# Far-attention stores moved from SyncE's queue to GpSimd's, and larger yields in the attention stream of a merged transformer layer

## The chip, the cores and the metric

The kernel runs on one core of one Trainium2 chip. The metric is the device time of one execution in microseconds (us), lower is better. The engines are named as in the profile: PE (TensorE, with PEld for its weight loads), DVE (VectorE), ACT (ScalarE), POOL (GpSimd) and SP (SyncE, which here only issues transfers). Each engine works through its own instructions in order.

## The reference

One layer over a prompt of 2048 tokens and a sample of 32 tokens with a cache of 2048. Attention has 8 heads of 64 and is of the stick-breaking kind; a state-space mixer runs beside it, and a gated feed-forward part follows. Cut to what matters here:

```
z = einsum("bqhd,bkhd->bhqk", q, k) * HEAD_DIM ** -0.5
log_beta = log_sigmoid(z);  log_1mb = where(k_pos < q_pos, log_beta - z, 0)
after = reverse_cumsum(log_1mb) - log_1mb
attn  = where(mask, exp(log_beta + after), 0) @ v
mixed = concat([rms_norm(attn), rms_norm(ssm)]) @ w_out      # output projection
x  = x + gate1 * mixed
h2 = rms_norm(x) * (1 + scale2) + shift2
x  = x + gate2 * ((silu(h2 @ w_gate) * (h2 @ w_up)) @ w_down)
```

A key far from its query usually gets almost no weight, since the product of the factors between them has gone to zero. The kernel uses that (next section).

## The kernel before, in words

All products run in two halves: `split` (lines 58 to 60) makes a high part on ACT (line 59) and the rest on DVE or POOL (line 60), and `mm3` (lines 130 to 132) issues three matmuls for each block. Weights are loaded in pieces of 1 MB into `wr`, and split into `wh` and `wl`; POOL does the rest part for most of them.

After the input projection, two streams are written as Python generators and interleaved by `merge`.

- Stream A is attention and output projection. For the prompt's token groups 1 to 3 (512 tokens each) it does windowed attention over the last keys (`attn_w`), which stores its output to `aoD` in HBM. `far_keys` then picks out the few rows of queries (at most 128, over all heads) whose keys beyond the window still have weight, gathers these queries (line 521, the only transfer that POOL issues in the kernel), and passes over 7 chunks of 256 keys: 16 matmuls into `fz` (line 575), sigmoids and scan, two transposes (line 594), 8 matmuls into `facc` (line 602). Each chunk loads 2 MB of keys (`Kf`) and 1 MB of values (`Vf`). At its end the result is spread into `OZ` (DVE, lines 609 to 619) and added into the stored rows: for each group g, `arows(g)` loads four tiles of 128x512 of `aoD` into two buffers (`aof`, two tiles to a buffer), two matmuls per tile (`far`, line 642) select the rows, DVE adds (line 643), and `store` writes the tile back to `aoD`. With two buffers, the next group's loads reuse them.
- Then stream A does `project(g)` for g = 1, 2, the sample and g = 3: `Wout.pre` loads the state-space half of the input (`mH`, `mL`), the gate rows `gr`, the residual rows `x1` (the profile shows the name as `x`) and pieces of `w_out`; `ssm` and `run` form `z` (12 matmuls per block of 128 tokens), scale it into `tm` with `gr` (DVE, line 761), add on POOL (line 763), norm (`norm2`, with a POOL power at line 150, `xn`, and PE transposes at line 825), and store `h2D`. The tiles of `project` lie where the tiles of the far part lay.
- Stream F is the feed-forward part, `ffn(g)` for g = 0 to 3, with 11 pieces for each group: `pg` and `pu` (24 matmuls each, twice), then `py` (8 blocks of 6 matmuls). In the last piece POOL also does the residual work (lines 923 and 924). Before the `py` of the last piece it yields `("need", g + 1)`, and loads the next group's input `h` (16 loads of 256 KB from `h2D`).

Every `yield c` of stream A adds `c * ratio` to a debt, and stream F is advanced until its own yields have paid it. The ratio is 1.55 and becomes 4.0 after `project(1)`. If F needs a group that A has not finished, A alone is advanced until it has. What results is the order of emission; a list scheduler then sets the final order of each engine, so that the matmuls of F may still move to where A would wait. Loads and stores go through `load` and `store`, both on SP's queue: a store there that waits for DVE holds back every load behind it.

Of the kernel before, what the change touches and what calls it, by code (L numbers as in the profile page):

```python
# [35 lines left out]
def body(tc, nc, I, O):  # L36
    V, A, G, PE = nc.vector, nc.scalar, nc.gpsimd, nc.tensor
    ctx = ExitStack()
    with ctx:
# [15 lines left out]
        def store(dst, src):  # L55
            nc.sync.dma_start(dst, src)

        def split(h, l, src, eng=None):
            A.activation(h, src, AF.Copy)  # L59
            (eng or V).tensor_tensor(l, src, h.bitcast(F32), op=ALU.subtract)  # L60
# [114 lines left out]
        aoD = dr.tile([NQ, 4, P, 512], F32, name="aoD")  # L175
# [12 lines left out]
        def zps(name="z"):  # L188
            return pz.tile([P, 512], F32, tag="z", name=name)
# [263 lines left out]
        def far_keys(at_, aT, L):  # L453
# [93 lines left out]
            def kget():  # L547
                if klist:
                    cb, hp = klist.pop(0)
                    Ks = at_.tile([P, 2, 640], F32R, tag="Kw", name="Kf", bufs=2).rearrange("p a t -> p (a t)")[:, :1024].rearrange("p (h a t) -> p h a t", h=2, a=2)  # L550
                    for h2 in range(2):
                        for i in range(2):
                            load(Ks[i * 64:(i + 1) * 64, h2].bitcast(F32), KT[:, hp, h2 * 64:h2 * 64 + 64, cb * 256:cb * 256 + 256].rearrange("a p t -> p a t"))
                    kq.append(Ks)
# [12 lines left out]
            for ci, cb in enumerate(range(nc_ - 1, -1, -1)):  # L567
                c0 = cb * 256
                z = zps("fz")[:, 0:256]
                for hp in range(4):  # L570
                    Ks = kq.pop(0)
                    for h2 in range(2):
                        hd = hp * 2 + h2
                        for a in range(2):
                            PE.matmul(z, lhsT=Qz[hd // 4][:, hd % 4, :], rhs=Ks[:, h2, a, :], start=(hd == 0 and a == 0), stop=(hd == 7 and a == 1))
                    kget()
                    yield 480
                a_ = aT[1][:, 1, :]
                b = t512("b", "fb")[:, 0:256]
                A.activation(a_[:, :256], z, AF.Sigmoid, scale=-1.0)  # L580
                A.activation(b, z, AF.Sigmoid)
                lim = tl("lim", 1)
                V.tensor_scalar(lim, tw[:, 1:2], -float(c0), None, op0=ALU.add)
                V.scalar_tensor_tensor(a_[:, :256], c["io"], lim, a_[:, :256], op0=ALU.is_ge, op1=ALU.max)
                V.scalar_tensor_tensor(b, c["io"], lim, b, op0=ALU.is_lt, op1=ALU.mult)
                Pt = t512("P", "fP")[:, 0:258]
                V.tensor_tensor_scan(Pt[:, 0:257][:, ::-1], a_[:, ::-1], cd[:, ::-1], 0.0, op0=ALU.mult, op1=ALU.add)
                if cb > 0:
                    V.tensor_copy(cd[:, 256:257], Pt[:, 0:1])
                V.tensor_tensor(b, b, Pt[:, 1:257], op=ALU.mult)  # L590
                yield 2500
                t = tps()
                for kb in range(2):
                    PE.transpose(t[:, kb * P:(kb + 1) * P], b[:, kb * P:(kb + 1) * P], ident)
                hh = at_.tile([P, 512], F32R, tag="hh", name="fh", bufs=2)
                ll = at_.tile([P, 512], F32R, tag="ll", name="fl", bufs=2)
                split(hh[:, :256], ll[:, :256], t[:, :256])
                for kb in range(2):
                    for hs in range(2):
                        Vs = vq.pop(0)  # L600
                        for a, wt in enumerate((hh, ll)):
                            PE.matmul(acc[hs], lhsT=wt[:, kb * P:(kb + 1) * P], rhs=Vs, start=(ci == 0 and kb == 0 and a == 0),
                                      stop=(cb == 0 and kb == 1 and a == 1))
                        vget()
                        yield 500
# [25 lines left out]
            for g in range(1, NQ):  # L631
                aos = arows(g)
                V.tensor_scalar(tq, c["bk"], tw[:, 2:3], 512.0 * g, op0=ALU.subtract, op1=ALU.add)
                V.tensor_scalar(tq, tq, -1.0, None, op0=ALU.mult)
                S2 = t512("b", "S2", F32R)
                V.tensor_tensor(S2.rearrange("p (j s) -> p j s", j=4), c["io"][:, 0:P].unsqueeze(1).to_broadcast([P, 4, P]),
                                tq.unsqueeze(2).to_broadcast([P, 4, P]), op=ALU.is_equal)
                yield 3000
                for hp in range(4):
                    ps = tps("far")  # L640
                    for i in range(2):
                        PE.matmul(ps, lhsT=OZ[i][:, hp * P:(hp + 1) * P], rhs=S2, start=(i == 0), stop=(i == 1))
                    V.tensor_tensor(aos[hp], ps, aos[hp], op=ALU.add)
                    store(aoD[g, hp], aos[hp])
                    yield 460

        def attn_s(at_, near):

# [346 lines left out]
        def project(g, pool):  # L995
            w = Wout(g, pool, zps)
            w.pre()
            yield 3000
            yield from w.ssm()
            yield from w.run()  # L1000

# [597 lines left out]
        with ExitStack() as pb_:  # L1599
            mp = pb_.enter_context(tc.tile_pool(name="mp", bufs=1))  # L1600
            mHL, stat = mixed(mp)
            pw0 = ExitStack()
            w0 = Wout(0, pw0.enter_context(tc.tile_pool(name="wo0", bufs=1)), dense_ps)
            w0.pre()
            merge2(a0, w0.ssm(), R1)
            pa0.close()
            fc = px_.enter_context(tc.tile_pool(name="fc", bufs=1, side="right"))
            far_consts(fc)
            L = fc.tile([P, NH, 12], F32, name="L")
            px1 = ExitStack()  # L1610
            at1 = px1.enter_context(tc.tile_pool(name="at1", bufs=1, side="right"))
            wt = window_tiles(at1)
            a1 = chain(*(attn_w(g, at1, L, wt) for g in range(1, NQ)))
            run_all(w0.run())
            pw0.close()
            fp = pb_.enter_context(tc.tile_pool(name="fp", bufs=1))
            late = {}

            def streamA():
                yield from a1  # L1620
                yield from far_keys(at1, wt[0], L)
                px1.close()
                for g in range(1, NQ):
                    if g == 3:
                        yield from part_s()
                    with tc.tile_pool(name=f"wo{g}", bufs=1, side="right") as wo:
                        yield from project(g, wo)
                    if g < 3:
                        yield ("done", g)
                    if g == 1:  # L1630
                        yield ("ratio", 4.0)
                px_.close()
                late["ex"] = pb_.enter_context(tc.tile_pool(name="ex", bufs=1, side="right"))
                dpool[0] = pb_.enter_context(tc.tile_pool(name="pdF", bufs=5, space=PSUM))
                yield ("done", 3)

            def streamF():
                hT = load_h(0, fp, None)
                for g in range(NQ):
                    hT = yield from ffn(g, fp, late, hT)  # L1640

            merge(streamA(), streamF(), 1.55)


        fx = ctx.enter_context(tc.tile_pool(name="fx", bufs=1))
# [54 lines left out]
def merge(a, f, ratio):  # L1700
    done, debt = set(), 0.0
    a_live, f_live, need = True, True, None
    while a_live or f_live:
        blocked = a_live and need is not None and need not in done
        if not blocked:
            need = None
        if a_live and (blocked or not f_live or debt <= 0):
            try:
                c = next(a)
                if isinstance(c, tuple) and c[0] == "ratio":  # L1710
                    ratio = c[1]
                elif isinstance(c, tuple):
                    done.add(c[1])
                elif not blocked:
                    debt += c * ratio
            except StopIteration:
                a_live = False
        else:
            try:
                c = next(f)  # L1720
                if isinstance(c, tuple):
                    need = c[1]
                else:
                    debt -= c
            except StopIteration:
                f_live = False
# [29 lines left out]
```

## Time and profile before

| | |
|---|---|
| median of 3 runs | 2940.25 us (2933.54 to 2941.23) |
| profiled execution | 2940.34 us, its span 2938.4 us |
| PE busy | 2729.8 us (93% of the span) |
| DVE, ACT, POOL busy | 1563.9, 1186.0 and 1532.6 us |
| instructions | 41844 |
| read from HBM, written to it | 372.66 MB, 91.04 MB |

In the profile, a group or timeline row names the engine, the source line, the operation, its output and inputs, and how many; a bracket behind it tells how long the engine had idled and what ended the wait. "SPq" is SP's transfer queue. Rows of windows give busy time of each engine in a stretch, the granted clock of PE as a share of full speed (PEclk), the busy share of the DMA engines, and GB/s. Line numbers are those of the kernel before; behind line 597 those of the changed kernel are one higher.

### The profile page before, as it was taken

How to read it: one execution, taken by the hardware profiler on the slowest of the kernel's cores; microseconds unless marked ns; L12 is line 12 of the kernel's file. 1: busy time of each engine (PE TensorE's matmuls, PEld its weight loads, DVE VectorE, ACT ScalarE, POOL GpSimd, SP SyncE). 2: the span in 40 equal slices, each digit the busy share in tenths (PEclk: the TensorE clock that was granted, in tenths of full speed). 3: DMA queues.
4: the chain of work that ended last, by engine and by line, in shares of the span. 5: the costliest groups of instructions: out<-in, count | busy, mean ns of one | idle time of the engine just before them, and what ended most of it. 6: DMA issues, size and time to landing. Idle time of an engine off the chain costs nothing.

```text
span 2938.4 us, 41844 instructions
## 1 busy us (share of the span) xinstructions
PE 2729.8 (93%) x15467; PEld 2334.2 (79%) x15467; DVE 1563.9 (53%) x2575; ACT 1186.0 (40%) x2533; POOL 1532.6 (52%) x1318
## 2 busy tenths in 40 slices
PE   6998998998978689998879999999999999999998
PEld 5988997896977578876667887777787788899997
DVE  6577586766568567874344534434434422333336
ACT  6466365555535455522224334333243422322221
POOL 4767566564654635743136655544564445544445
PEclk8999998999988789999989999999999999999999
DMA  8755653463467787837745744534733722422221
GB/s 266 219 171 153 202 177 114 119 182 106 131 175 237 193 225 196 208 116 213 199 165 180 258 135 137 152 122 155 236 127 106 230 88 92 154 87 87 86 87 66
DMA packets 415619, 466.54 MB, mean 159 GB/s; under 512 B 34191, under 2 KB 330991, under 8 KB 415406
## 3 DMA queue, kind: packets, MB, share of 16 engines
q1 hardware_dynamic: 414478, 463.61, 52.7%
q8 instruction: 124, 2.03, 0.3%
q14 instruction: 89, 0.73, 0.1%
q10 hardware_dynamic: 896, 0.14, 0.0%
q0 software_dynamic: 32, 0.03, 0.0%
HBM read 372.66 MB, written 91.04 MB: 158 GB/s over the span
## 4 chain that ended last, share of the span: by engine, by line
PE 57%; DVE 6%; DMA 5%; issue 3%; POOL 2%; ACT 2%; SPq 1%; DVEq 0%; ACTq 0%; POOLq 0%
PE pg L130 5%; PE pg L131 5%; PE pg L132 5%; PE pu L130 5%; PE pu L131 5%; PE pu L132 5%; PE py L130 5%; PE py L131 4%; PE py L132 4%; PE z L130 2%; PE z L131 2%; PE z L132 1%; PE d L131 1%; PE d L130 1%; PE d L132 1%
## 5 line engine op out<-in xcount | busy, mean ns | idle before, releaser
L60 POOL TENSOR_TENSOR wl<-wr,wh 128x512 fp32r<-128x512 f32 x752 | 1010.3, 1375 | 861.7 <-ACT wh L59 778.5
L59 ACT ACTIVATE wh<-wr 128x512 fp32r<-128x512 f32 x816 | 450.3, 620 | 512.3 <-PE py L132 128.4
L130 PE MATMUL d<-wh,hH 128*128 128x256 f32 (+2 forms) x1088 | 316.0, 291 | 18.8 <-ACT hH L59 10.9
L132 PE MATMUL d<-wh,hL 128*128 128x256 f32 (+2 forms) x1088 | 311.8, 287 | 6.7 <-POOL hL L60 6.7
L130 PE MATMUL pg<-h,wh 128*128 128x512 f32 (+1 forms) x880 | 311.3, 354 | 3.7 <-POOL aT L378 2.5
L130 PE MATMUL pu<-h,wh 128*128 128x512 f32 (+1 forms) x880 | 310.5, 353 | 1.2 <-DVE sg L952 1.2
L131 PE MATMUL d<-wl,hH 128*128 128x256 f32 (+2 forms) x1088 | 311.4, 286 | 0.0
L132 PE MATMUL pg<-h,wl 128*128 128x512 f32 (+1 forms) x880 | 310.7, 353 | 0.6 <-POOL wl L60 0.6
L131 PE MATMUL pg<-h,wh 128*128 128x512 f32 (+1 forms) x880 | 310.7, 353 | 0.0
L132 PE MATMUL pu<-h,wl 128*128 128x512 f32 (+1 forms) x880 | 310.5, 353 | 0.0
L131 PE MATMUL pu<-h,wh 128*128 128x512 f32 (+1 forms) x880 | 309.9, 352 | 0.0
L130 PE MATMUL py<-wh,aH 128*128 128x512 f32 x704 | 282.5, 401 | 7.0 <-DVE ya L983 5.0
L131 PE MATMUL py<-wl,aH 128*128 128x512 f32 x704 | 277.0, 394 | 0.0
L983 DVE TENSOR_TENSOR ya<-py,ya 128x512 f32<-128x512 f32 x288 | 190.4, 684 | 148.4 <-PE py L132 146.8
L132 PE MATMUL py<-wh,aL 128*128 128x512 f32 x704 | 265.8, 394 | 2.8 <-DVE aL L60 2.8
L952 DVE TENSOR_TENSOR sg<-pg,sg 128x512 f32<-128x512 f32 (+1 forms) x110 | 64.8, 589 | 336.8 <-ACT sg L951 336.8
L130 PEld LDWEIGHTS d<-wh,hH 128*128 128x128 f32 (+1 forms) x1088 | 207.7, 191 | 23.2 <-ACT hH L59 12.5
L132 PEld LDWEIGHTS d<-wh,hL 128*128 128x128 f32 (+1 forms) x1088 | 206.9, 190 | 8.0 <-POOL hL L60 7.2
L131 PEld LDWEIGHTS d<-wl,hH 128*128 128x128 f32 (+1 forms) x1088 | 207.3, 191 | 0.7
L130 PEld LDWEIGHTS pg<-h,wh 128*128 128x128 f32 x880 | 165.6, 188 | 28.5 <-POOL aT L378 2.7
L130 PEld LDWEIGHTS pu<-h,wh 128*128 128x128 f32 x880 | 165.5, 188 | 24.2 <-DVE sg L952 1.4
L132 PEld LDWEIGHTS pg<-h,wl 128*128 128x128 f32 x880 | 165.4, 188 | 24.1 <-POOL wl L60 1.1
(434 smaller groups left out, 5686.7 us busy)
## 6 DMA issues: line engine op xcount, KB each, us to landing
wr<-in_w_in SPq DMA_DIRECT2D x48, 1024.0 KB
wr<-in_w_gate SPq DMA_DIRECT2D x44, 1024.0 KB
wr<-in_w_up SPq DMA_DIRECT2D x44, 1024.0 KB
wr<-in_w_down SPq DMA_DIRECT2D x44, 1024.0 KB
wr<-in_w_ada SPq DMA_DIRECT2D x24, 1024.0 KB
wr<-in_w_out SPq DMA_DIRECT2D x20, 1024.0 KB
h2D<-hl SPq DMA_DIRECT2D x64, 256.0 KB
Kw<-KT SPq DMA_DIRECT2D x48, 320.0 KB
```

Of the source, the lines that this page charges most:

```text
L59: A.activation(h, src, AF.Copy)
L60: (eng or V).tensor_tensor(l, src, h.bitcast(F32), op=ALU.subtract)
L130: PE.matmul(out, lhsT=sh, rhs=mh, start=(i == 0), stop=False)
L131: PE.matmul(out, lhsT=sh, rhs=ml, start=False, stop=False)
L132: PE.matmul(out, lhsT=sl, rhs=mh, start=False, stop=(i == n - 1))
L952: V.tensor_tensor(sg[:, :n], pg[:, :n], sg[:, :n], op=ALU.mult)
L983: V.tensor_tensor(dst, ps[:r], dst, op=ALU.add)
```

## The change

Stores of the far part's rows are issued by POOL (`G.dma_start`) and not by SP. Five numbers that rule the interleaving are changed: the yield behind a far chunk's scan from 2500 to 3500; a new yield of 1500 between the split of its weights and the value matmuls; 460 to 800 behind each far row tile; 3000 to 5000 behind the loads of `project`; and the first ratio of `merge` from 1.55 to 1.5.

```diff
                 V.tensor_tensor(b, b, Pt[:, 1:257], op=ALU.mult)
-                yield 2500
+                yield 3500
                 t = tps()
...
                 split(hh[:, :256], ll[:, :256], t[:, :256])
+                yield 1500
                 for kb in range(2):
...
                     V.tensor_tensor(aos[hp], ps, aos[hp], op=ALU.add)
-                    store(aoD[g, hp], aos[hp])
-                    yield 460
+                    G.dma_start(aoD[g, hp], aos[hp])
+                    yield 800
...
             w = Wout(g, pool, zps)
             w.pre()
-            yield 3000
+            yield 5000
             yield from w.ssm()
...
-            merge(streamA(), streamF(), 1.55)
+            merge(streamA(), streamF(), 1.5)
```

What the scheduler makes of it. Through the first six far chunks PE's order is the same in both. On SP, from the row loads of the far part to the loads of `project(1)`, there stands before:

```order
L53 DMA wr<-in_w_up 128x8x256
L53 DMA Vf<-VS 128x512 x2
L56 DMA aoD<-aof 128x512 x4
L53 DMA aof<-aoD 128x512 x4
L56 DMA aoD<-aof 128x512 x4
L53 DMA aof<-aoD 128x512 x4
L56 DMA aoD<-aof 128x512 x4
L53 DMA gr<-modD 128x4x128 x2
```

and now on SP:

```order
L53 DMA Vf<-VS 128x512 x2
L53 DMA wr<-in_w_out 128x4x512
L53 DMA wr<-in_w_gate 128x8x256
L53 DMA aof<-aoD 128x512 x4
L53 DMA wr<-in_w_up 128x8x256
L53 DMA aof<-aoD 128x512 x4
L53 DMA gr<-modD 128x4x128 x2
```

with the stores on POOL, between weight splits and the adds of `project(1)`:

```order
L60 TENSOR_TENSOR wl<-wr,wh 128x512 x40
L645 DMA aoD<-aof 128x512 x12
L764 TENSOR_TENSOR x_15879<-x_15879,tm 128x512
L764 TENSOR_TENSOR x_15881<-x_15881,tm 128x512
L764 TENSOR_TENSOR x_15883<-x_15883,tm 128x512
L60 TENSOR_TENSOR wl<-wr,wh 128x512
```

The twelve stores have left SP. The loads of `aof` for the next group still wait for the landing of the stores out of the buffer they reuse, and the first `gr` load waits for the landing of the last stores, as before. Two weight loads (`in_w_gate`, `in_w_up`) now stand ahead of `gr`.

On PE at the same place, before, all 24 `far` matmuls follow each other, with one `z` block ahead and the next behind:

```order
L132 MATMUL z<-wh,mL 128x512
L642 MATMUL far<-S_15471,OZ 128x512 x8
L642 MATMUL far<-S_15529,OZ 128x512 x8
L642 MATMUL far<-S_15603,OZ 128x512 x8
L130 MATMUL z<-wh,mH 128x512
```

and now the first group's 8 are split, with 18 `py` matmuls between them and 12 behind (first and last rows of it):

```order
L643 MATMUL far<-S_15575,OZ 128x512 x4
L130 MATMUL py<-wh,aH 128x512
L131 MATMUL py<-wl,aH 128x512
L132 MATMUL py<-wh,aL 128x512
```

```order
L132 MATMUL py<-wh,aL 128x512
L643 MATMUL far<-S_15575,OZ 128x512 x4
L130 MATMUL py<-wh,aH 128x512
```

```order
L132 MATMUL py<-wh,aL 128x512
L643 MATMUL far<-S_15687,OZ 128x512 x8
L643 MATMUL far<-S_15775,OZ 128x512 x8
L130 MATMUL z<-wh,mH 128x512
```

From the last `facc` matmul to the first `far` there is one block of 12 `z` before; now these 12 `z` stand among 22 matmuls of F (4 `pu` and 18 `py`). In all, 120 matmuls of F that came later stand ahead of the last `far` now: 52 of them behind the last `facc`, the rest in the last chunk.

The third place is the end of `project(1)`, where stream F goes from token group 0 to group 1. On PE, behind the last transposes of `norm2`, before:

```order
L825 MATMUL t<-ident,xn 128x128 x8
L132 MATMUL pu<-h_11612,wl 128x512
L130 MATMUL pu<-h_11613,wh 128x512
L131 MATMUL pu<-h_11621,wh 128x512
L132 MATMUL pu<-h_11613,wl 128x512
```

and now:

```order
L826 MATMUL t<-ident,xn 128x128 x8
L130 MATMUL pg<-h_17041,wh 128x512
L130 MATMUL pu<-h_17041,wh 128x512
L130 MATMUL pg<-h_17041,wh 128x512
L131 MATMUL pg<-h_17049,wh 128x512
```

`h_116..` are the tiles of group 0, `h_170..` of group 1. Before, 165 matmuls of group 0 and of `project(2)` stand between the last transposes and the first `pg` of group 1; now none does. `h_17041` and `h_17049` are the first and the fifth of the 16 loads that SP issues behind the last `h2D` stores.

## Prediction

> **What bounds the kernel now.** I read the page's first lines, then the stretches of 100 us, and then the chain of waits inside the one stretch that stood out.
>
> ```profile
> span 2938.4 us, 41844 instructions
> PE 2729.8 (93%) x15467; PEld 2334.2 (79%) x15467; DVE 1563.9 (53%) x2575; ACT 1186.0 (40%) x2533; POOL 1532.6 (52%) x1318
> 1300.00:1400.00 100.00, 91.32 (x424) 72.71 (x423) 40.77 (x65) 24.17 (x49) 37.11 (x28) 1.00 0.67 180
> 1400.00:1500.00 100.00, 75.01 (x287) 56.10 (x286) 40.00 (x72) 13.29 (x27) 7.66 (x7) 0.82 0.72 218
> 1500.00:1600.00 100.00, 98.49 (x450) 80.38 (x448) 45.05 (x68) 41.84 (x85) 54.11 (x44) 0.99 0.41 132
> 1600.00:1700.00 100.00, 98.74 (x428) 79.39 (x429) 57.89 (x69) 36.51 (x71) 67.08 (x49) 0.98 0.79 262
> 2700.00:2800.00 100.00, 100.00 (x690) 93.32 (x690) 33.93 (x64) 25.23 (x57) 35.70 (x29) 1.00 0.27 85
> ```
>
> PE carries the kernel; its work is the same after the change, so the time moves by what PE loses: idle time, and matmuls at a lowered clock. The far part (1300 to 1500 us) is where it loses: 9 us idle in the first of these stretches, 25 in the second, there with the clock at 0.82. Around 1650 us, where F goes from group 0 to group 1, it loses next to nothing. These are the two places that the change touches.
>
> The chain of waits in the far rows:
>
> ```profile
> 1464.28 0.70 DVE om L609
> ...
> 1472.13 0.69 DVE aof L643
> 1472.84 2.12 DMA aoD<-aof
> 1475.03 2.66 DMA aof<-aoD
> 1477.81 0.70 DVE aof L643
> 1478.56 2.09 PE far L642 x4
> ...
> 1481.96 2.10 DMA aoD<-aof
> 1484.13 3.53 DMA aof<-aoD
> ...
> 1489.16 2.10 DMA aoD<-aof
> 1491.33 3.81 DMA gr<-modD
> 1495.27 0.76 DVE tm L761
> 1496.08 0.79 PE z L130
> 1496.87 0.43 PE z L131
> ...
> 1501.56 0.37 PE z L130
> 1502.63 0.24 PE z L131
> ```
>
> Three rounds of add, store, load, and then `gr`: each load waits for a store to have landed, since it reuses the buffer (and `gr` the far part's memory). A matmul takes 0.43 us while the clock is low and 0.24 at full clock. From 1464.28 to 1501.56, 37.3 us, PE does 12 `z`, 24 `far` and 12 `z` matmuls: 48 x 0.24 = 11.5 us of work, so 25.8 us are lost there.
>
> **Term 1, the far rows.** Three parts of this stretch change.
>
> Before the first `far`, DVE makes `OZ`:
>
> ```profile
> 1463.65 1.32 DVE L609 TENSOR_TENSOR om<-facc,oh 128x512 f32<-128x512 f32 x2 [3.07 <-PE facc L602]
> 1469.28 0.68 DVE L619 TENSOR_TENSOR OZ<-Ohl,oh 128x512 fp32r<-128x512 f32 x1
> 1597.25 0.75 DVE L115 SCALAR_TENSOR_TENSOR wl<-wr,cols,wh 128x512 fp32r<-128x512 f32 x1
> ```
>
> That takes 6.3 us. In the new order DVE does six more instructions in it (four of line 115 at 0.75, two of F on 128x512 like `OZ`, 0.68): 4.4 us, so the first `far` stands 10.5 us behind `om`, not 6. If they fit into DVE's waits it is bounded by PE's 34 matmuls there, 8 us.
>
> The stores. Here is what the trace has for a store by SP, and the one transfer that POOL issues, a gather:
>
> ```profile
> L56 SPq DMA_DIRECT2D aoD<-aof x12: 319/320/320, 1472.2 to 1489.2; - x12
> L521 POOL DMA_INDIRECT Qg<-Qn,ix x1: 1216/1216/1216, 1295.0 to 1295.0; - x1
> DMA to landing us min/median/max: 4.0/4.0/4.0
> ```
>
> No row shows a plain store issued by POOL. The ends are a store like SP's (0.32 to issue, 2.1 to land) and one like the gather (1.2 and 4.0). I take the gather's issue, since it is the engine's own price, and SP's remainder for the same 256 KB (2.1 - 0.3 = 1.8): 3.0 to land. A round needs both stores of a buffer, whose adds end 0.65 apart: last landing at 0.65 + 2.1 = 2.75 behind the first add with SP, at 1.2 + 1.2 + 1.8 = 4.2 with POOL. That is 1.45 more, three times: 4.4 us (0 to 7.4 with the two ends). SP is not needed for anything in this time that PE could use: what stands behind the stores, `gr`, waits for their landing anyway. So taking the stores off SP frees nothing here. Behind the stores on POOL stand the adds of `project(1)`, which need `gr` too, and then a weight split whose first use on PE is behind three `z` blocks; nobody waits for it first.
>
> The Trainium skill (DMA: Bandwidth & Descriptors, anatomy of one DMA) gives a transfer issued by GpSimd as about 2.0 us plus its bytes at 436 GB/s, an estimate of 2.6 us for 256 KB; by that the three rounds would cost some 1.5 us more than SP's 2.1, and the forecast would come 3 us lower; no row of this trace shows such a store. The same page says under "Issuing engines are not separate DMA queues" that issuing from several engines only saves the sequencer's time; that speaks against a gain from the move, as the chain above does.
>
> The `py` matmuls between the first group's `far` halves (18 x 0.24 = 4.3 us) put off its second pair of stores; the chain shows that this pair then waited for PE anyway (2.09 us of `far` at the low clock), so not all of it counts, and I add 1 us, an estimate. From the first `far` to the next `z` it took 25.8 us (1470.3 to 1496.1); I get 31 (26.5 to 34). Then 12 `z` at the low clock, 5.2.
>
> Sum: 10.5 + 31 + 5.2 = 46.7 us against 37.3, 9.4 longer. But 52 matmuls of F now lie inside, 52 x 0.24 = 12.5 us that need not be done later: **-3.1 us**, with the ends 39.7 - 37.3 - 12.5 = -10.1 and 49.9 - 37.3 - 12.5 = +0.1.
>
> **Term 2, the last chunk.** Through six chunks PE's order is the same, and the chunks' loads too, so I cost their stalls at no change. In the last chunk, 68 matmuls of F are added ahead of the last `facc`, 24 of them ahead of its last `fz`. They can cover these waits:
>
> ```profile
> 1440.00:1450.00 10.00, 7.52 (x32) 5.82 (x31) 2.74 (x5) 2.85 (x6) 4.26 (x4) 0.86 0.95 287
> 1447.04 0.69 PE L575 MATMUL fz<-Kf,Qz 128*128 128x256 f32 x2 [2.10 <-DMA Kf<-KT]
> 1462.89 0.50 PE L602 MATMUL facc<-Vf,fh 128*128 128x512 f32 x1 [2.73 <-DMA Vf<-VS]
> ```
>
> 2.5 us idle and 1.0 of low clock (7.52 x 0.14) in the first, 2.7 in the second: at most 6.2. The queue is at 0.95 of its bandwidth in there and the new matmuls need weights over it, so **-5 us**, between -6.2 and 0.
>
> **Term 3, from group 0 to group 1.** Larger yields let F run further ahead of A: F now comes to its request for group 1 before `project(1)` has finished, and the scheduler has used up the rest of group 0 (48 `py`) while the last two blocks were normed. Behind the last transposes of `norm2` PE's next instruction needs `h` of group 1. Before, 165 matmuls stood there (165 x 0.24 = 40 us), and covered this chain:
>
> ```profile
> L825 PE MATMUL t<-ident,xn x16: 270/272/273, 1597.5 to 1624.6; 128*128 128x128 f32 x16
> 1630.97 0.36 SPq L56 DMA_DIRECT2D h2D<-hl  x1
> 1632.62 0.81 SPq L53 DMA_DIRECT2D h<-h2D  x2
> 1638.56 11.82 SPq L53 DMA_DIRECT2D h<-h2D  x14
> ```
>
> Last transposes at 1624.6, then ACT and DVE make `hl`, SP stores it (last at 1630.97), and the first `h` load is issued at 1632.62: 8.0 us. The load lands 2.66 later (the row of `aof`, the same 256 KB). Three matmuls can run with the first tile; the next needs the fifth load, four issues of 11.82 / 14 = 0.84 later: 3.4, less 3 x 0.24. Idle: 8.0 + 2.7 + 3.4 - 0.7 = 13.4 us. From there the loads come at 1.7 us for a pair, and 9 matmuls of `pg`, `pu` and `pg` (2.2 us) wait for each pair, so they flow. PE starts at the low clock, 12 matmuls at 0.43 as at 1496: 12 x 0.19 = 2.3. **+15.7 us.** At the least it is 8.0 + 2.7 = 10.7, since PE works in order and has nothing else; at the most 24, with POOL late (below).
>
> The ratio of 1.5 and the yield of 5000 in later projects cost nothing by my reading: F's matmuls cover them there, as they do now (98.5 and 98.7 us busy in the two stretches behind 1500), and the next two loads of `h` still stand well ahead of their first use. PE's reserve is the part with F alone at the end (100 us busy of 100), which gets shorter by what F is ahead.
>
> **Sum.** -3.1 - 5 + 15.7 = +7.6 us on the profiled execution's 2940.3 us (span 2938.4 and 1.9 around it; the median shown is the same to 0.1): **2948 us**. The ends: -10.1 - 6.2 + 10.7 = -5.6 and +0.1 + 0 + 24 = +24.1, so 2934 to 2964.
>
> **Rivals.**
> *The far rows' stall is filled (faster).* The new F matmuls, whose weights are loaded ahead, could take up all of the 25.8 us: 15.7 - 25.8 - 5 = -15, 2925 us. For it speaks that POOL, ACT and PE are all nearly idle there, so the room is there. Against it: 16 `far` matmuls stand in a row on PE with no F between, and a `z` behind, whose two buffers wait for `gr`. It decides if what is lost there falls under 6 us, which needs the chain of three stores to be hidden.
> *POOL is late (slower).* In the last piece of group 0 POOL does 16 residual instructions, and the norm's power stands behind them:
>
> ```profile
> 1610.58 3.88 POOL L923 TENSOR_TENSOR ya<-ya,gr 128x512 f32<-128x512 f32 x3
> 1617.37 1.00 POOL L150 TENSOR_TENSOR rsd<-rs,mhalf 128x1 f32<-128x1 f32 x1
> ...
> L60 POOL TENSOR_TENSOR wl<-wr,wh 128x512 fp32r<-128x512 f32 x752 | 1010.3, 1375 | 861.7 <-ACT wh L59 778.5
> ```
>
> 16 x 1.3 = 21 us, with five weight pieces of 4 x 1.375 = 5.5 us and eight adds of 1.3: about 58 us of POOL against some 60 of PE in the new order. If POOL falls 8 us behind, the last transposes do too, with nothing for PE: 24 for term 3, 2956 us. For it: the balance is that tight. Against: POOL idles several times there now.
> *Little changes.* If term 3 is at its low end and the other two at theirs, 2935 to 2940 us. Against it, all three must come out low.
>
> **How the numbers follow.** I give the forecast (2941 to 2955) 0.48, POOL late 0.22, little changes 0.18, the filled stall 0.12. A difference of 0.3%, 8.8 us, is about what a measurement of this kernel can tell. The forecast at +7.6 lies just under it, so it goes half to "same" (0.24) and half to "slower". Faster 0.12; same 0.24 + 0.18 = 0.42; slower 0.24 + 0.22 = 0.46. The range of 2934 to 2964 leaves out the filled stall and a longer delay on POOL.
>
> **What would show it.** Term 3: a wait of 10 us or more on PE for `h<-h2D` behind the last transposes of `project(1)`, with a granted clock under 1 in that stretch. Term 1: the store rows on POOL with more than 2.1 us to land, and a `z` that still waits for `tm` and `gr` about 31 us behind the first `far`. Term 2: no wait for `Vf` ahead of the last `facc`. I am wrong if PE has work at the change of groups, or if the `gr` load no longer comes last.

## The result, and the profile after

The changed kernel takes 2962.88 us (median of 4 runs, 2961.86 to 2964.16), the kernel before 2939.65 beside it: 1.0071 times as long, 95% interval 1.0054 to 1.0089. The profiled execution took 2964.16 us, its span 2962.4, which is 24.0 us more than before. The first lines of its page, and the stretches of 100 us:

```profile
span 2962.4 us, 41849 instructions
PE 2732.0 (92%) x15467; PEld 2336.6 (79%) x15467; DVE 1560.7 (53%) x2575; ACT 1185.4 (40%) x2533; POOL 1537.9 (52%) x1330
1400.00:1500.00 100.00, 89.34 (x383) 69.39 (x381) 44.76 (x82) 21.40 (x41) 19.54 (x20) 0.94 0.67 195
1500.00:1600.00 100.00, 85.84 (x375) 69.45 (x376) 30.62 (x49) 24.42 (x47) 58.65 (x49) 0.90 0.39 135
1600.00:1700.00 100.00, 78.76 (x333) 62.15 (x332) 45.59 (x64) 39.39 (x84) 46.27 (x37) 0.88 0.80 260
2100.00:2200.00 100.00, 95.28 (x401) 76.15 (x402) 37.73 (x53) 34.38 (x66) 49.35 (x39) 0.97 0.55 184
```

PE's busy time grew by 2.2 us only; the rest of the 24 is idle time. The far part's loss has moved from 1400:1500 into 1500:1600 and became smaller, and 1600:1700, which lost 1.3 us before, is now idle for 21.2. The stretch 2100:2200 is new: the kernel before had there

```profile
2100.00:2200.00 100.00, 99.92 (x448) 80.93 (x447) 36.19 (x52) 36.20 (x68) 62.45 (x49) 1.00 0.48 164
```

From here on "loss" is PE's idle time plus its busy time times (1 - granted clock), summed over stretches of 10 us. It finds 26.9 us more after than before, where the spans differ by 24.0; for the other kernels below, it meets the difference of the spans to within 10 us. Ahead of 1300 us the loss is 2.4 lower after than before. The far part (1300 to 1600) went from 46.3 to 38.7, the change from group 0 to group 1 (1600 to 1700) from 2.9 to 26.2, and 1700 to 2600 from 11.3 to 24.8, of which 2000 to 2200 from 3.3 to 13.6.

The chain of waits in the far rows, as shown of before:

```profile
1489.35 3.50 DMA aoD<-aof
1493.36 4.02 DMA aof<-aoD
1497.48 0.70 DVE aof L644
1498.46 5.82 DMA aoD<-aof
1504.70 3.35 DMA aof<-aoD
1508.14 0.70 DVE aof L644
1509.12 2.29 DMA aoD<-aof
1511.66 3.65 DMA gr<-modD
1515.43 0.76 DVE tm L762
1516.24 0.80 PE z L130
```

The three rounds of add, store and load are there as before, and `gr` still comes last. One store took 5.82 us to land. Ahead of this chain, in the timelines of DVE and PE:

```profile
1471.90 1.39 DVE L610 TENSOR_TENSOR om<-facc,oh 128x512 f32<-128x512 f32 x2 [1.68 <-PE facc L603]
1480.86 1.34 PE L643 MATMUL far<-S,OZ 128*128 128x512 f32 x4
```

The second `om` starts at 1471.90 + 1.39 / 2 = 1472.6, the first `far` 8.3 us behind it.

PE at the change from group 0 to group 1 (a row with a bracket tells the idle time ahead of it), and SP's queue there:

```profile
1643.53 0.63 PE L826 MATMUL t<-ident,xn 128*128 128x128 f32 x4 [2.67 <-DVE xn L819]
1644.94 0.63 PE L826 MATMUL t<-ident,xn 128*128 128x128 f32 x4 [0.79 <-DVE xn L819]
1658.15 0.79 PE L130 MATMUL pg<-h,wh 128*128 128x512 f32 x1 [12.58 <-DMA h<-h2D]
1662.00 0.79 PE L131 MATMUL pg<-h,wh 128*128 128x512 f32 x1 [2.20 <-DMA h<-h2D]
```

```profile
1643.30 4.16 SPq L56 DMA_DIRECT2D h2D<-hl  x4
...
1650.01 2.91 SPq L56 DMA_DIRECT2D h2D<-hl  x4
1655.14 9.17 SPq L53 DMA_DIRECT2D h<-h2D  x16
```

After its last transposes PE waits 12.58 us for the first tile of `h` and 2.20 for the fifth. And PE had waited for `xn` before that. `xn` needs `rsd`, which POOL makes as a power of `rs`. DVE and POOL ahead of it:

```profile
1638.34 0.14 DVE L149 TENSOR_SCALAR rs<-s 128x1 f32<-128x1 f32 x1
1638.40 1.28 DVE L987 TENSOR_TENSOR yt<-py,gr 128x512 f32<-128x512 f32 x2
1639.60 2.38 DVE L988 TENSOR_TENSOR ya<-ya,yt 128x512 f32<-128x512 f32 x2
1641.90 2.90 DVE L819 TENSOR_SCALAR xn<-x,rsd 128x512 f32<-128x512 f32 x2
```

```profile
1637.61 1.96 POOL L925 TENSOR_TENSOR ya<-ya,xf 128x512 f32<-128x512 f32 x1 [4.70 <-DMA xf<-x1D]
1639.52 1.30 POOL L60 TENSOR_TENSOR wl<-wr,wh 128x512 fp32r<-128x512 f32 x1
1640.76 1.02 POOL L150 TENSOR_TENSOR rsd<-rs,mhalf 128x1 f32<-128x1 f32 x1
```

The norm's `rs` is ready at 1638.5. On DVE four residual instructions of stream F (`yt`, `ya`) stand between it and `xn`, until 1642.0. On POOL the power stands behind a residual add, which had waited 4.70 us for its `xf`, and behind a weight split; it ends at 1641.8. Either of the two was enough to hold `xn` until then.

### The profile page after: what moved, and what is told of

Its sections match the earlier page's. It is cut to its first block, busy times and chain, and to the rows that moved or that the text cites. A ratio compares the mean times of both kernels' runs of the same rounds, so it can differ in the third digit from the quotient of the medians.

```text
span 2962.4 us, 41849 instructions
## 1 busy us (share of the span) xinstructions
PE 2732.0 (92%) x15467; PEld 2336.6 (79%) x15467; DVE 1560.7 (53%) x2575; ACT 1185.4 (40%) x2533; POOL 1537.9 (52%) x1330
## 4 chain that ended last, share of the span: by engine, by line
PE 58%; DVE 6%; DMA 5%; issue 2%; POOL 2%; ACT 2%; SPq 0%; DVEq 0%; POOLq 0%; ACTq 0%
PE pg L130 5%; PE pg L131 5%; PE pg L132 5%; PE pu L131 5%; PE pu L130 5%; PE pu L132 5%; PE py L130 5%; PE py L131 5%; PE py L132 4%; PE z L130 1%; PE z L131 1%; PE z L132 1%; PE d L131 1%; PE d L130 1%; POOL wl L60 1%
## 5 line engine op out<-in xcount | busy, mean ns | idle before, releaser
L130 PEld LDWEIGHTS pg<-h,wh 128*128 128x128 f32 x880 | 166.6, 189 | 45.0 <-DMA h<-h2D 12.8
L131 PEld LDWEIGHTS pg<-h,wh 128*128 128x128 f32 x880 | 166.7, 189 | 26.3 <-DMA h<-h2D 2.9
L130 PEld LDWEIGHTS pu<-h,wh 128*128 128x128 f32 x880 | 165.7, 188 | 24.8 <-DVE sg L953 2.0
```

The source lines that it names most:

```text
L130: PE.matmul(out, lhsT=sh, rhs=mh, start=(i == 0), stop=False)
L131: PE.matmul(out, lhsT=sh, rhs=ml, start=False, stop=False)
```

## The experiments

My theory (A) is that F, put ahead of A in the far part, has nothing left where A makes the input of group 1, and that what A is late there it is late at later changes too. Rivals: the stores on POOL cost the time (B); DVE and POOL are late with the residual adds whatever PE has left (C).

Each kernel was timed beside the kernel before, on the same chip. This table gives what they have in common: how many matmuls stand on PE between the last `norm2` transposes ahead of it and the first `pg` of the new group (the cover), the loss at that place, and the loss of the far part. At the change from group 1 to group 2 the transposes counted are those of the sample's 32 rows.

| kernel | ratio to before (95%) | cover 0 to 1 | loss 1600 to 1700 | cover 1 to 2 | loss 2000 to 2200 | loss 1300 to 1600 |
|---|---|---|---|---|---|---|
| before | 1 | 165 | 2.9 | 87 | 3.3 | 46.3 |
| changed | 1.0071 (1.0054 to 1.0089) | 0 | 26.2 | behind it | 13.6 | 38.7 |
| stores alone | 1.0018 (1.0000 to 1.0035) | 165 | 2.6 | 87 | 5.4 | 49.9 |
| numbers alone | 1.0086 (1.0066 to 1.0106) | 0 | 25.8 | behind it | 11.9 | 37.5 |
| far yields alone | 1.0042 (1.0028 to 1.0057) | 0 | 27.3 | 66 | 10.6 | 33.6 |
| yield of project alone | 1.0049 (1.0034 to 1.0064) | 131 | 1.2 | 66 | 15.4 | 42.7 |
| changed, project 3000 | 1.0043 (1.0028 to 1.0058) | 0 | 22.8 | 66 | 10.8 | 39.5 |
| changed, first ratio 1.4 | 1.0031 (1.0016 to 1.0045) | 73 | 4.6 | 66 | 12.8 | 39.7 |
| far yields, then ratio 1.2 | 1.0009 (0.9994 to 1.0025) | 47 | 10.3 | 70 | 11.1 | 35.9 |
| changed, then ratio 1.2 | 1.0058 (1.0044 to 1.0073) | 36 | 12.4 | 0 | 24.5 | 44.4 |
| changed, then ratio 0.8 | 0.9967 (0.9955 to 0.9980) | 217 | 0.3 | 87 | 3.8 | 45.7 |
| far yields, then ratio 0.8 | 0.9946 (0.9928 to 0.9964) | 229 | 0.0 | 280 | 0.0 | 45.6 |
| changed, `xf` by POOL | 1.0151 (1.0132 to 1.0170) | 0 | 33.5 | 0 | 25.4 | 41.3 |
| before, then ratio 0.8 | 1.0037 (1.0022 to 1.0052) | 429 | 3.8 | 446 | 0.0 | 60.1 |

"Then" is from the end of the far part to the end of `project(1)`.

The losses are those of one profiled execution for each kernel, and they scatter. PE's order up to the last `far` is the same in the kernel before and with the yield of `project` alone, and from 1300 to 1530 us they lost 44.7 and 41.6 us. It is the same in the changed kernel, with `project` at 3000 there and with the two later ratios there, and these lost 38.6, 39.4, 44.0 (ratio 1.2) and 39.9 (0.8). A difference of 5 us in the last column says little.

**Stores or numbers.** The kernel before with `store(aoD[g, hp], aos[hp])` written `G.dma_start(aoD[g, hp], aos[hp])`, and the changed kernel with that line put back.

> The kernel before with one edit: the twelve far-row stores are issued by POOL. PE's order stays that of the kernel before. Theory A (stream A falls behind stream F, the change from group 0 to group 1 is left without cover): this edit alone is worth little, 2938 to 2945 us; three rounds of store and load get up to 1.4 us longer each. Theory B (the stores on POOL are what costs, by a longer landing and by holding up POOL's work behind them): 2955 us or more. In both the store rows show 0.54 us to issue and about 3.5 to land.

> The changed kernel with the stores back on SP, so the five numbers alone. PE's order is that of the changed kernel. Theory A: 2957 to 2964 us, with the wait of about 15 us for h at the change of groups still there. Theory B: 2935 to 2948.

The stores alone: 2948.22 us against 2944.75, 0.18% with an interval that touches none. Without them the five numbers cost 0.86% (2967.09 us). Both times lie some 3 us above the ranges given for theory A, but the kernel before was 5 us slower in this comparison than in the first. So the numbers carry the loss, and theory B falls. The stores issued by POOL, in the kernel with them alone:

```profile
L644 POOL DMA_DIRECT2D aoD<-aof x12: 539/539/618, 1476.8 to 1495.2; - x12
DMA to landing us min/median/max: 2.3/2.7/3.2
```

and in the changed kernel, where a weight load of F ran beside them:

```profile
L645 POOL DMA_DIRECT2D aoD<-aof x12: 539/539/616, 1484.7 to 1509.1; - x12
DMA to landing us min/median/max: 2.3/3.5/6.1
```

That the 5.82 us in the chain is not POOL's doing shows in the chain of the numbers alone, where SP issued the same store:

```profile
1497.64 6.27 DMA aoD<-aof
```

In both kernels SP had issued the 1 MB of `in_w_up` shortly before, at 1494.83 and 1495.66. In the changed kernel that load moved from 1496.4 to 1501.8 us, and the packets of the two stores issued at 1497.15 and 1498.46 only from 1500.3 to 1503.9.

**Which number.** The three far yields alone in the kernel before; the yield of `project` alone in the kernel before; the changed kernel without that yield:

```diff
-                yield 2500
+                yield 3500
...
                 split(hh[:, :256], ll[:, :256], t[:, :256])
+                yield 1500
...
-                    yield 460
+                    yield 800
```

```diff
             w.pre()
-            yield 3000
+            yield 5000
```

> The kernel before with the three far yields alone (3500, 1500, 800); ratio 1.55, the later yield of 3000 and the stores on SP stay. No matmul covers the change from group 0 to group 1, as in the changed kernel; ahead of group 2 the order is that of neither (66 matmuls behind the last norm2 transposes, against 87 before and 852 in the changed kernel). Theory A: the change of groups loses 20 to 27 us as in the changed kernel, the far part gains 6 to 12. If the loss of 13 us between 1700 and 2600 follows from the change of groups, it stays, and the time is 2955 to 2965; if it follows from where the later projects stand, it goes, and the time is 2945 to 2953.

> The kernel before with one edit: the yield behind the loads of every project is 5000 and not 3000. 131 matmuls stand at the change from group 0 to group 1 (165 before, none in the changed kernel); ahead of group 2 the order is 66 matmuls instead of 87. Theory A: far part and change of groups cost what they cost before (46 and 3 us of PE's loss). For the loss between 1700 and 2600 us (11 before, 25 in the changed kernel): if the larger yield causes it, it is 18 or more here and the time is 2946 to 2955; if it follows from the late change of groups, it is 9 to 14 and the time is 2938 to 2945.

> The changed kernel with the yield of project back at 3000. No matmul covers the change from group 0 to group 1, as in the changed kernel. Theory A: that change still loses 20 to 27 us, the far part as in the changed kernel. If the yield of 5000 causes the loss between 1700 and 2600 us, it falls from 25 to 9 to 15, and the time is 2948 to 2955; if the loss follows from the change of groups, it stays at 20 or more, and the time is 2957 to 2965.

The far yields alone lose 27.3 us at the change of groups, and gain 12.7 in the far part: both the gain and the larger loss are theirs. The yield of `project` alone keeps the first change covered and loses 15.4 us from 2000 to 2200; taking it out of the changed kernel gives back 0.28%, with intervals that overlap. By that, it seemed to cause the later loss by itself. The changed kernel with the ratio at 0.8, below, corrects this.

**Giving the cover back.** If the loss is what the matmuls at the change of groups leave uncovered, less of F ahead of it must bring the time back. First with the first ratio:

```diff
-            merge(streamA(), streamF(), 1.5)
+            merge(streamA(), streamF(), 1.4)
```

> The changed kernel with the first ratio at 1.4 and not 1.5, so that stream F gets less of its work done before project(1) has finished. 73 matmuls (48 py of group 0, 24 z) now stand between the last norm2 transposes and the first pg of group 1, where the changed kernel has none; that is 17.5 us of work against a chain of about 14. Theory A: PE's loss from 1600 to 1700 us falls from 26 to under 6, the losses behind it (2050 to 2470) fall too since project(2) comes at another place, and the time is 2932 to 2945. Rival C (DVE and POOL are late with the residual adds of the last piece, whatever PE has left): the adds stand in the same place, the transposes still wait for xn, and more than 12 of the 26 us stay: 2948 to 2960.

The loss there fell from 26.2 to 4.6, and the rival C with it: DVE still does the residual adds at this place, and PE does not wait for long. But the later loss stayed, 25.0 us from 1700 to 2600, and the time of 2953.01 lies above the range given. So the second half of theory A does not hold: here, and with the yield of `project` alone (1.2 and 25.2), the change to group 1 costs little and the later loss is as large as in the changed kernel. The next two lower the ratio only behind the far part, in the kernel before with the far yields and in the changed kernel:

```diff
                 yield from far_keys(at1, wt[0], L)
+                yield ("ratio", 1.2)
```

> The kernel before with the three far yields (3500, 1500, 800), and the ratio set to 1.2 behind the far part until project(1) is done; stores on SP, yield of project 3000. 217 matmuls cover the change from group 0 to group 1, 524 of F stand ahead of the last far as in the changed kernel. Theory A (what was lost is the cover that F had used up): far part 33 to 40 us of loss against 46 before, change of groups under 5, and the time 2928 to 2942, so faster than before or equal to it. If the far part's gain is paid back elsewhere (project(1) waits with less of F between its steps), 2943 to 2955.

> The changed kernel with one edit: the ratio is set to 1.2 (from 1.5) behind the far part until project(1) is done. PE's order up to the last far is that of the changed kernel; 217 matmuls now stand at the change from group 0 to group 1, and 87 ahead of group 2 as in the kernel before. Theory A: the loss at the change of groups falls from 26 to under 5, the far part keeps its gain. If the loss between 1700 and 2600 us comes from the late change of groups, it goes as well and the time is 2930 to 2940; if it comes from the yield of 5000, it stays and the time is 2941 to 2950.

The counts of cover in these two texts (217 and 87) are wrong: the orders have 47 and 70 in the first, 36 and 0 in the second, as the table says (and the first has 548 matmuls of F ahead of the last `far`, not 524). So the second came out slow, against every number written for it, and yet as the theory has it for the change to group 1: with 36 matmuls of cover, PE waits again, though less than with none.

```profile
PE pg L130 <- DMA h<-h2D: 2.9, 1, 2.9
PE py L130 <- DVE yt L987: 2.8, 2, 2.5
PE z L130 <- DVE tm L762: 1.5, 1, 1.5
PE pg L131 <- DMA h<-h2D: 1.1, 1, 1.1
```

(The waits of PE from 1600 to 1700 us there; in the changed kernel the first was 12.58.) Not all of the loss at partial cover is a wait for `h`: here these are 4.0 us, and in the first of the two, with 47, only 0.6, beside 4.3 that the profile puts down to a weight split on DVE. With 0.8 in place of 1.2 the counts are as large as meant:

> The changed kernel with one edit: the ratio is set to 0.8 (from 1.5) behind the far part until project(1) is done. As with 1.2, but now 217 matmuls stand at the change from group 0 to group 1 (with 1.2 it was 36 and not the 217 that was written there), and 87 ahead of group 2. Theory A (the loss at the change of groups is what the matmuls there leave uncovered): 26 us falls to under 4, the far part stays at 36 to 42. The loss between 1700 and 2600 us stays at 18 or more, since the yield of 5000 does, and the time is 2936 to 2947. If what F no longer does in project(1) is missed there, 1550 to 1650 us loses 5 us or more and the time is 2947 or above.

> The kernel before with the three far yields (3500, 1500, 800) and the ratio set to 0.8 behind the far part until project(1) is done; stores on SP, yield of project 3000. 229 matmuls cover the change from group 0 to group 1 (47 with the ratio at 1.2), 280 stand ahead of group 2. Theory A: far part 33 to 40 us of loss against 46, change of groups under 4, 1700 to 2600 us 11 to 18; 2928 to 2940, so faster than before or equal. If project(1) now waits for want of F's matmuls, 2940 to 2952.

One number behind the far part turns the changed kernel from 0.71% slower into 0.33% faster, 2931.43 us. With the stores on SP and `project` at 3000 it is 2927.78 against 2941.86, 0.54% faster than the kernel before: the best version here. Its stretches:

```profile
1500.00:1600.00 100.00, 85.19 (x366) 68.35 (x367) 39.10 (x67) 36.98 (x80) 43.34 (x35) 0.87 0.50 167
1600.00:1700.00 100.00, 100.00 (x451) 81.54 (x450) 46.52 (x61) 38.31 (x72) 68.67 (x52) 1.00 0.75 248
2100.00:2200.00 100.00, 100.00 (x448) 81.39 (x447) 33.67 (x47) 36.11 (x68) 54.64 (x42) 1.00 0.43 140
```

PE is busy through both changes of groups. In the profiled executions its span is 14.0 us under that of before: 8.2 less idle time (200.4 against 208.6) and 5.8 less busy time (2724.0 against 2729.8). The loss by stretches sees only some 5 of these 14, so where in the program the gain lies is not settled. The far part kept less of its gain than the two texts expected (45.6 and 45.7 us for 33 to 42): 7.3 and 5.7 us of that lie behind 1530, where `project(1)` waits, 2.6 us of it for `tm`. Both times came out below the ranges given.

And the changed kernel with 0.8 still has `project` at 5000, and loses 3.8 us from 2000 to 2200 and 10.5 from 1700 to 2600, where 18 or more was expected. So the yield of `project` is not the cause by itself. What it changed in the kernel before is the order: 66 matmuls ahead of group 2 in place of 87.

**Two that went another way.** In the changed kernel PE's longest wait behind 2000 us is

```profile
2121.43 0.79 PE L130 MATMUL pg<-h,wh 128*128 128x512 f32 x1 [4.70 <-DVE yt L987]
```

`yt` stands on DVE behind a residual add that waits for POOL's add of `xf`. SP issued a load of `xf` at 2119.88, behind the sample's stores of `h2D`, and I took that for the cause. So I let POOL issue the loads of `xf` (`G.dma_start` in place of `load`):

> The changed kernel with one edit: the loads of xf (the residual rows in the last piece of each group) are issued by POOL and not by SP, so that they no longer stand behind the loads of h and the stores of h2D on SP's queue. POOL adds each xf itself, from a single buffer. PE's order is that of the changed kernel up to group 1 (still no cover there), and differs somewhat behind it. If the waits between 2000 and 2200 us (13.6 us of loss) come from xf's place in SP's queue, they fall to under 6, and the time is 2948 to 2957; if they come from the larger yield in another way, they stay at 11 or more, and the time is 2958 to 2968. In both the change to group 1 still loses 20 or more.

The loss from 2000 to 2200 rose from 13.6 to 25.4 and the time to 2986.79. On POOL, the add of `xf` stands behind weight splits:

```profile
2103.93 0.55 POOL L915 DMA_DIRECT2D xf<-x1D  x1
...
2112.91 9.92 POOL L60 TENSOR_TENSOR wl<-wr,wh 128x512 fp32r<-128x512 f32 x8 [5.09 <-ACT wh L59]
2122.79 1.26 POOL L925 TENSOR_TENSOR ya<-ya,xf 128x512 f32<-128x512 f32 x1
```

The load was issued at 2103.9, and its add came at 2122.8, behind eight splits of weights. The sample's norm moved up to the change of groups in this kernel too, with 0 matmuls of cover, and its loss is that of the other kernel with 0 (24.5).

The changed kernel's own trace shows that SP's queue was not the cause of that wait. The load at 2119.88 belongs to a later add, at 2125.07. The `xf` of the add that `yt` waited for had been issued at 2102.80, and the chain of waits does not pass through it:

```profile
2110.01 0.38 PE t L826 x4
2110.47 0.98 ACT hx L832 x4
...
2112.93 0.53 ACT wh L59
2113.59 5.05 POOL wl L60 x4
2118.64 1.23 POOL ya L925
2119.89 0.70 DVE ya L988
2120.68 0.70 DVE yt L987
2121.43 0.79 PE pg L130
```

It starts at the sample's `norm2`. Its transposes stand on PE behind 24 `pg` of group 2. ACT, which works in order, waited 5.5 us for them to make `hx`, and F's weight split stands behind `hx` on ACT; POOL's part of the split, its residual add, DVE and PE follow. The kernels with the numbers alone, with the ratio of 1.2 in the changed kernel, and with `xf` by POOL have the same chain there, and PE waits 4.7, 9.8 and 15.4 us at its end. In the kernel before, ACT did not wait for the sample's transposes, and PE waits 1.2 us at most. This is read from traces; no run took one link of the chain away.

Last, the ratio of 0.8 without the far yields, to see whether they earn anything:

> The kernel before with one edit: the ratio is set to 0.8 (from 1.55) behind the far part until project(1) is done; far yields, yield of project and stores as before. It has the cover at the changes of groups (429 matmuls at 0 to 1, 446 at 1 to 2) without the far part's larger yields: 380 matmuls of F stand ahead of the last far, against 404 before and 524 with the far yields. Theory A gives: far part 44 to 49 us of loss, change of groups 0 to 1 about 0 (3 before), 1700 to 2600 us 6 to 11 (11 before), so 2930 to 2940, 4 us or more behind the run with the far yields and the same ratio. If the ratio alone made that run fast and the far yields earn nothing even with cover, this one comes out at 2920 to 2929.

It came out above both ranges, 2954.65 against 2944.47. The changes of groups are covered as expected, and F is now missing where A waits: the far part loses 60.1 us, and `project(1)` has a wait of 6.6 us for `tm` behind 1590. So the ratio alone doesn't make the fast version. With the far yields, the same ratio gives 0.9946, without them 1.0037: the two edits work only together.

## Why the prediction was right, and where its sizes were off

The forecast was +7.6 us with a range of -6 to +24; the spans differ by +24.0, and the medians by 23. The direction held, and so did the mechanism that decides the sum: F's cover at the change to group 1 is used up, PE waits there for `h`, and the far rows give back less than that costs. The size is three times the forecast. That it still lies in the range, 1 us from its end at 2964, is luck: a place that was costed at nothing lost 13.5 us more, and the range had no room made for it.

- **Term 1 and Term 2**, -8.1 in all, came out at -7.6 (46.3 to 38.7), within the scatter said above. From `om` to the first `far` it took 8.3 us (10.5 forecast, 6 before); from the first `far` (1480.86) to the next `z` (1516.24) 35.4, above the upper end of 34. The issue on POOL was 0.54 us, not the gather's 1.2, and the landing in the kernel with the stores alone 2.7, near the 3.0 taken. What was missed is the 5.82: a store beside F's weight load lands late whoever issues it (6.27 from SP). The 12 `z` behind took 4.5 us and not 5.2, since the clock was back after seven of them. By the same sum, 8.3 + 35.4 + 4.5 - 37.3 - 12.5, Term 1 is -1.6. (The forecast's upper end for it was summed 0.2 too high: 10.5 + 34 + 5.2 is 49.7.) Ahead of `om`, from 1300 us on, the loss fell from 20.4 to 15.5 us (in stretches of 2 us), the -5 of Term 2. The waits for `Vf`, 5.5 us in two places, are gone, the last one as said; those for `Kf` only went from 10.0 to 9.5, with one of 4.7 in place of the two that the term had counted on. The rival that the stall is filled is out: from `om` on some 23 us are still lost. The Trainium skill's advice (DMA: Bandwidth & Descriptors, "Issuing engines are not separate DMA queues") agrees with the run of the stores alone, 1.0018: the move to POOL gained nothing. The estimate of 2.6 us for such a store from the Trainium skill (the same page, anatomy of one DMA) stands beside a median of 2.7 there.
- **Term 3** was +15.7 and measured +23.3 (2.9 to 26.2), just under the end given as 24. The wait behind the last transposes was well sized: 12.58 + 2.20 = 14.8 against 13.4; transposes to first load took 9.6 (8.0), the load 3.0 (2.7), the fifth tile 2.2 (2.7). What the sum lacked lies ahead of it and beside it: 3.5 us of waiting for `xn`, 2.8 idle from 1620 to 1630, and 5.0 of low clock instead of 2.3. 14.8 + 3.5 + 2.8 + 5.0 = 26.1. The rival "POOL is late" had a part of this: the norm's power did stand behind POOL's residual work, and began 2.3 us behind `rs`. But POOL was not short of time, it had waited 4.7 us for `xf`; and DVE's residual adds, which the rival did not name, held `xn` as long.
- **Costed at nothing, and wrong:** the later projects. "The next two loads of h still stand well ahead of their first use" was true, and beside the point. From 1700 to 2600 the loss grew by 13.5 us. Stream A's sample block came to stand on the last piece of group 1, behind the first `pg` of group 2 in PE's order. The runs show how this goes with the order: 280 or 446 matmuls of cover there lose 0, 87 lose 3.3 to 5.4, 66 to 70 lose 10.6 to 15.4, 0 loses about 25; with the transposes behind the first `pg`, as in the changed kernel, it is 12 to 14. Group 2 needs only what `project(2)` stored long before, so this is no wait for `h`. For the longest wait the traces show the way: the sample's transposes hold up ACT, ACT the weight split of F, and that POOL's residual, DVE and PE. No experiment took one link away alone, and the shorter waits there, as 2.75 us for `ya` at 2055, have other chains; so the cause of the whole 13.5 stays open.

The sum by the measured sizes is -7.6 + 23.3 + 13.5 = 29.2; less the 2.4 by which the loss ahead of 1300 us fell it is 26.8, and the spans differ by 24.0, so the estimate of losses counts some 3 us too much.

## What to carry to other kernels

When two streams share an engine, work put ahead as filler is taken from somewhere: count what is left at the next place where the filler's own input is made, before counting the gain. At the change to group 1, the more matmuls stood between the producer's last step and the consumer's first, the less was lost: 23 to 33 us with none, 12 with 36, 10 with 47, 5 with 73 (17.5 us of work), 0 to 4 with 131 or more. And a yield that works can be paid for by a second number: here more filler in the far part and less of it in the stage behind, neither of which helps alone.

## What the runs showed of the hardware

A store of 256 KB issued by POOL held POOL for 0.54 us and landed in 2.3 to 3.2 us where no weight load ran beside it; SP's took 0.32 and 2.1. Beside a weight load of 1 MB the same stores took up to 6.1 us from POOL and 6.27 from SP. At the change of groups the DMA engines were fully taken:

```profile
1640.00:1650.00 10.00, 2.11 (x12) 1.21 (x10) 7.08 (x6) 7.13 (x19) 5.92 (x5) 0.79 1.08 348
1650.00:1660.00 10.00, 1.65 (x3) 0.83 (x3) 1.29 (x2) 0.63 (x1) 0.00 (x0) 0.50 1.05 327
1660.00:1670.00 10.00, 8.00 (x26) 6.41 (x27) 0.00 (x0) 0.00 (x0) 0.00 (x0) 0.69 1.07 369
```

PE's clock was still at 0.69 in the 10 us after it had work again. These 30 us alone hold 18.2 us of idle time and 3.7 of low clock (2.11 x 0.21 + 1.65 x 0.50 + 8.00 x 0.31).
